# Ten root sums a layer on GpSimd, lagged sums on GpSimd, two mixer outputs parked in DRAM, and one squared root in the convolution

## The chip, the cores and the metric

The kernel runs on one core of one Trainium2 chip. The metric is the device time of one execution in microseconds (us). Three runs of the kernel before took 2062.20, 2062.73 and 2065.04 us; their median is 2062.73 us.

## The reference

A decoder trunk of two layers over 1024 tokens of width 1024, all in float32. Cut to what matters here (`norm` divides by the root of the mean square over the last axis):

```python
for l in range(2):
    h = rmsnorm(x, attn_norm[l])
    (c_q, c_kv, k_r, g_b, g_c, u_conv, u_pool, q_sw, k_sw, v_sw) = split(h @ w_in[l])
    y_a = mla_attention(c_q, c_kv, k_r, ...)      # RMSNorm of c_q and of c_kv inside
    y_b = g_b * conv3(g_c * u_conv)               # causal, depthwise, width 3
    y_c = pool(u_pool) @ pool_w * pool_scale      # trailing means over 2, 4, 8, 16 tokens
    y_d = swa_sink_attention(q_sw, k_sw, v_sw)    # window of 128 tokens
    mixed = concat(norm(y_a), norm(y_b), norm(y_c), norm(y_d)) * mix_norm[l]
    x = x + mixed @ w_o[l]
    gate, up = split(rmsnorm(x, ffn_norm[l]) @ w_gate_up[l])
    x = x + (silu(gate) * up) @ w_down[l]
return rmsnorm(x, final_norm)
```

## The kernel before

Channels lie on the 128 partitions, tokens on the free axis in two halves t of 512. To keep float32 accuracy, each operand of a product is split in two float32r parts (ScalarE casts the high part, VectorE subtracts it), and `mm3` (L260) issues three matmuls for each product of tiles. SBUF beside constants and temporaries is 47 slots of 128 x 1024 (`u`), handed out and taken back by `Slots`.

**One layer, in the order of the code.** The projections of the local attention (group d), the first half of the convolution (group b), the pooling (group c: its lagged sums are `lagged`, L770 to L785), the low-rank q and kv projections with their norms (`sq_q` at L822, `sq_kv` at L832), the second half of the convolution (`conv(1)`), which serves as TensorE work while the keys and queries of the main attention (group a) are made, then eight attention steps with pieces of the output projection (`out_some`) between them, then the feed-forward part.

**The norms.** The class `SumSq` (L298) squares tiles on ScalarE and adds them on VectorE. `rnorm` (L334) sums the result over the 128 partitions with a matmul against a matrix of ones: one plain float32 matmul (L343), or, with `pair=True`, the sum is first split in two and there are two float32r matmuls (L340). The product lies in PSUM on all partitions; three ScalarE operations (L349 to L351) and two of VectorE (L352, L355) make the inverse root. A layer has ten such sums inside the mixers: two halves each for groups b, c and d (`group_scale`, L673), for `sq_q` and for `sq_kv`. Of them b and kv use the pair. Group a, the two norms of x and the final norm use `rnorm` too.

**What sets the order.** Nothing runs in the order of the code. `scheduled_kernel` (L1972) traces the kernel, gives every instruction a cost (`Order.costs`), makes a list schedule for the five engines (PE, ScalarE, VectorE, GpSimd, SP with its DMAs), chooses PSUM banks from it, and fixes each engine's order by added dependencies. Each engine then takes its instructions strictly in that order: one that waits holds up all behind it. GpSimd runs the sums of feed-forward weights (L749 to L752 ahead of the attention, L1213 to L1243 and L1532 later), a multiplication in the gates (L1454) and small memsets (L1041).

Of the kernel before, what the change touches and what calls it, by code (L numbers as in the profile page):

```python
# [6 lines left out]

# [4 lines left out]

F32 = mybir.dt.float32
# [98 lines left out]
def trunk_kernel(ctx: ExitStack, tc: tile.TileContext, ins, out, given=None):  # L112
# [13 lines left out]
    def rd(ap):  # L126
        return ap.bitcast(F32)
# [170 lines left out]
    class SumSq:  # L298


        def __init__(self, n, pair=False):
            self.n, self.pair = n, pair
            self.acc = [None, None]
            self.done = {}
            self.held = {}
            self.hl = {}
# [27 lines left out]
        def rnorm(self, t, cols=whole, tag="t", final=None):  # L334

            a, n = F.ap(self.acc[t])[:, cols], self.n
            p = ps(tag)[:, cols]
            if t in self.hl:
                for i, h in enumerate(self.hl.pop(t)):
                    pe.matmul(p, ones_r, R.ap(h), start=i == 0, stop=i == 1)  # L340
                    R.free(h)
            else:
                pe.matmul(p, ones, a, start=True, stop=final is None)  # L343
# [8 lines left out]
            dve.scalar_tensor_tensor(  # L352
                out=q, in0=p, scalar=-0.5 / n, in1=q, op0=ALU.mult, op1=ALU.mult
            )
            dve.scalar_tensor_tensor(out=a, in0=q, scalar=1.5, in1=r0, op0=ALU.add, op1=ALU.mult)  # L355
            return self.acc[t]

    def mul_to(o, a, b):
# [2 lines left out]
    def pcol(l, c, rows=slice(0, P)):  # L361
        return par[rows, l * PC_N + c : l * PC_N + c + 1]
# [55 lines left out]
    for l in range(L):  # L418
# [115 lines left out]
        for t in range(2):  # L534
            f = tmp()
            mul_to(f, pk[t], r_of(t))
            for g, own, oth in ((0, hd, tl), (1, tl, hd)):
                k1, k2 = R.ap(kk[g][0] + t), R.ap(kk[g][1] + t)
                act.copy(k1[own], f[own])
                act.copy(k1[oth], f[own])  # L540
                dve.tensor_tensor(out=k2[own], in0=f[own], in1=rd(k1[own]), op=ALU.subtract)
                dve.tensor_tensor(out=k2[oth], in0=f[own], in1=rd(k1[own]), op=ALU.subtract)
        vs = [[R.half(), R.half()] for _ in range(2)]
        for t in range(2):
            f = tmp()
# [138 lines left out]

        mixed = {}

        def group_split(g, t):
            for c in range(2):
                s = y[g][c][t]
                mixed[g, c, t] = half_split(F.ap(s), pcol(l, PC_MIX + 2 * "abcd".index(g) + c))  # L690
                F.free(s)


        y["b"] = [None, None]

        def conv(ct):
# [13 lines left out]
            c = PC_CONV + ct  # L710
# [51 lines left out]
        for ct in range(2):  # L762
# [5 lines left out]
            nextp = project()  # L768

            def lagged(o, i, lag, rows=slice(0, P)):  # L770
                dve.tensor_copy(o[rows, :lag], i[rows, :lag])
                dve.tensor_tensor(
                    out=o[rows, lag:], in0=i[rows, lag:], in1=i[rows, : S - lag], op=ALU.add
                )

            lagged(af, uf, 1)
            if ct == 0:
                lagged(bf, af, 2, tl)
                dve.tensor_copy(bf[hd], af[hd])
                src, dst = bf, af  # L780
            else:
                lagged(bf, af, 2)
                lagged(af, bf, 4)
                lagged(bf, af, 8, tl)
                dve.tensor_copy(bf[hd], af[hd])  # L785
                src, dst = bf, af
            cf = CC_FIX + 16 * ct
            dve.scalar_tensor_tensor(
# [556 lines left out]
        for n, (h, t) in enumerate(steps):  # L1345
# [8 lines left out]
            if n == 0:  # L1354
# [450 lines left out]
class Order:  # L1805
# [74 lines left out]
    def costs(cls, i):  # L1880
# [320 lines left out]
```

## Time and profile before

| what | value |
|---|---|
| runs | 2062.20, 2062.73, 2065.04 us |
| span of the profiled execution, first to last instruction | 2061.2 us |
| median run less that span | 1.5 us |
| granted TensorE clock | 0.998 |
| mixers of layer 0 | about 0 to 235 us, attention steps to 440 us |
| mixers of layer 1 | about 1050 to 1235 us, attention steps to 1440 us |
| feed-forward parts | about 440 to 1050 us and 1440 to 2061 us |

The profile has no time of its own for the execution that it shows beside its span; what lies around the span is taken as the 1.5 us to the median. In its rows PE is TensorE, DVE VectorE, ACT ScalarE, POOL GpSimd and SP the queue that issues all DMAs. A row of instructions gives line, engine, operation, output<-inputs, shape, count, and busy time with the mean in ns. In the timeline a row begins with its start and its length in us. A float32 matmul stands as two records.

### The profile page before, as it was taken

How to read it: one execution, taken by the hardware profiler on the slowest of the kernel's cores; microseconds unless marked ns; L12 is line 12 of the kernel's file. 1: busy time of each engine (PE TensorE's matmuls, PEld its weight loads, DVE VectorE, ACT ScalarE, POOL GpSimd, SP SyncE). 2: the span in 40 equal slices, each digit the busy share in tenths (PEclk: the TensorE clock that was granted, in tenths of full speed). 3: DMA queues.
4: the chain of work that ended last, by engine and by line, in shares of the span. 5: the costliest groups of instructions: out<-in, count | busy, mean ns of one | idle time of the engine just before them, and what ended most of it. 6: DMA issues, size and time to landing. Idle time of an engine off the chain costs nothing.

```text
span 2061.2 us, 26597 instructions
## 1 busy us (share of the span) xinstructions
PE 2035.3 (99%) x9422; PEld 1673.6 (81%) x9422; DVE 1503.7 (73%) x2443; ACT 992.6 (48%) x1743; POOL 577.3 (28%) x420
## 2 busy tenths in 40 slices
PE   9999999999999999999999999999999999999998
PEld 7887888778888888888888878888788877788887
DVE  8779979987666667655657898889866655585555
ACT  7447657753333334444433666668433333354342
POOL 0200000037777773000002000000577777710000
PEclk9999999999999999999999999999999999999999
DMA  5211223334554556766413112142455555487642
GB/s 191 90 57 46 84 78 96 137 133 168 181 175 167 189 169 235 265 220 208 140 46 124 37 42 97 61 144 94 159 169 178 178 175 170 154 302 237 204 171 96
DMA packets 142118, 302.37 MB, mean 147 GB/s; under 512 B 13856, under 2 KB 60960, under 8 KB 141984
## 3 DMA queue, kind: packets, MB, share of 16 engines
q1 hardware_dynamic: 141984, 300.66, 43.1%
q8 instruction: 74, 1.21, 0.2%
q14 instruction: 60, 0.49, 0.1%
HBM read 212.00 MB, written 87.56 MB: 145 GB/s over the span
## 4 chain that ended last, share of the span: by engine, by line
PE 68%; POOL 7%; DVE 5%; DMA 4%; issue 2%; ACT 2%; SPq 0%; DVEq 0%; POOLq 0%; ACTq 0%
PE ps_mm L260 25%; PE ps_s L260 21%; PE ps_t L260 8%; PE ps_pv L260 6%; POOL u L1532 3%; PE ps_pv L1044 2%; PE ps_t L1032 1%; DMA u<-in_w_dn 1%; POOL tp L1454 1%; DMA ad<-u 1%; POOL u L1214 1%; DVE u L283 1%; POOL u L1213 1%; ACT u L280 1%; DMA u<-in_w_gu 1%
## 5 line engine op out<-in xcount | busy, mean ns | idle before, releaser
L260 PE MATMUL ps_mm<-u,u 128*128 128x512 f32 (+1 forms) x3378 | 831.0, 390 | 3.4 <-ACT u L280 2.3
L260 PEld LDWEIGHTS ps_mm<-u,u 128*128 128x128 f32 x3378 | 615.4, 188 | 130.4 <-issue 5.3
L260 PE MATMUL ps_s<-u,u 128*128 128x512 f32 x2670 | 636.1, 390 | 5.8 <-DVE tn L352 2.3
L283 DVE TENSOR_TENSOR u<-u,u 128x1024 fp32r<-128x1024 f32 (+2 forms) x400 | 443.3, 1126 | 225.2 <-ACT u L280 173.4
L260 PEld LDWEIGHTS ps_s<-u,u 128*128 128x128 f32 x2670 | 499.5, 188 | 117.8 <-ACT tn L1321 3.9
L280 ACT CAST u<-u 128x1024 fp32r<-128x1024 f32 (+2 forms) x400 | 345.1, 881 | 505.4 <-POOL u L1215 60.1
L260 PE MATMUL ps_t<-u,u 128*128 128x512 f32 (+1 forms) x1124 | 255.3, 378 | 2.8 <-DVE u L1447 2.7
L260 PEld LDWEIGHTS ps_t<-u,u 128*128 128x128 f32 x1124 | 201.6, 188 | 45.8 <-DVE u L1447 6.5
L1454 POOL TENSOR_TENSOR tp<-tp,u 128x512 f32<-128x512 f32 x80 | 135.1, 1689 | 341.7 <-ACT tp L1453 341.7
L260 PE MATMUL ps_pv<-u,u 128*128 128x512 f32 x744 | 177.8, 390 | 1.6 <-DVE te L1658 1.0
L260 PEld LDWEIGHTS ps_pv<-u,u 128*128 128x128 f32 x744 | 139.3, 188 | 32.1 <-ACT tn L1321 1.9
L1041 POOL MEMSET u<- 128x128 f32 x32 | 5.9, 211 | 472.9 <-PE ps_pv L1044 149.3
L1453 ACT ACTIVATE tp<-tp 128x512 f32<-128x512 f32 x80 | 50.5, 631 | 155.2 <-DVE tp L359 155.1
L749 POOL TENSOR_TENSOR u<-u,u 128x512 f32<-128x512 f32 x4 | 6.0, 1509 | 380.4 <-PE ps_t L622 288.9
L1532 POOL TENSOR_TENSOR u<-u 128x352 f32<-128x352 f32 x64 | 80.5, 1259 | 31.6 <-DMA u<-in_w_dn 30.2
L280 ACT CAST u<-ps_t 128x512 fp32r<-128x512 f32 (+3 forms) x132 | 65.1, 504 | 48.1 <-PE ps_t L1032 26.7
L1532 POOL TENSOR_TENSOR u<-u,u 128x352 f32<-128x352 f32 x64 | 85.0, 1328 | 3.0
L285 ACT ACTIVATE u<-u,par 128x512 fp32r<-128x512 f32 x100 | 70.6, 717 | 28.5 <-DVE u L359 11.1
L283 DVE TENSOR_TENSOR u<-ps_t,u 128x512 fp32r<-128x512 f32 (+3 forms) x132 | 75.9, 582 | 11.1 <-ACT u L280 9.8
L286 DVE SCALAR_TENSOR_TENSOR u<-u,par,u 128x512 fp32r<-128x512 f32 x100 | 73.7, 750 | 5.9 <-ACT u L285 5.9
L324 ACT ACTIVATE tn<-u 128x512 f32<-128x512 f32 (+1 forms) x91 | 52.3, 595 | 48.6 <-DVE u L1723 42.1
L359 DVE TENSOR_TENSOR tp<-tp,u 128x512 f32<-128x512 f32 x76 | 72.5, 954 | 2.0
(208 smaller groups left out, 2359.3 us busy)
## 6 DMA issues: line engine op xcount, KB each, us to landing
u<-in_w_gu SPq DMA_DIRECT2D x92, 512.0 KB, 4.1
ad<-u SPq DMA_DIRECT2D x154, 256.0 KB, 3.9
u<-ad SPq DMA_DIRECT2D x70, 512.0 KB, 5.1
u<-in_w_dn SPq DMA_DIRECT2D x64, 352.0 KB, 3.4
qd<-u SPq DMA_DIRECT2D x64, 352.0 KB, 2.4
u<-qd SPq DMA_DIRECT2D x32, 512.0 KB, 4.7
u<-in_w_in SPq DMA_DIRECT2D x28, 512.0 KB, 3.5
u<-in_w_dn SPq DMA_DIRECT2D x24, 512.0 KB, 5.2
```

What stands on the lines that cost most here:

```text
L260: pe.matmul(o, w, r, start=start and k == 0 and i == 0, stop=stop and k == n - 1 and i == 2, skip_group_check=again,)
L280: a = act.copy(hi, f)
L283: dve.tensor_tensor(out=lo, in0=f, in1=rd(hi), op=ALU.subtract)
L285: a = act.activation(hi, f, AF.Copy, scale=gain)
L286: dve.scalar_tensor_tensor(out=lo, in0=f, scalar=gain, in1=rd(hi), op0=ALU.mult, op1=ALU.subtract)
L324: act.activation(q, f, AF.Square)
L359: dve.tensor_tensor(out=o, in0=a, in1=b, op=ALU.mult)
L1032: pe.transpose(p[:, b * P : (b + 1) * P], pr[b][j // 4][:, (j % 4) * P : (j % 4 + 1) * P], ident,)
L1044: pe.matmul(py[:, c0:], v_of(j, h), R.ap(s)[:, c0:], start=j == 0 and n == 0, stop=j == nj - 1 and n == 1,)
L1453: last_silu = act.activation(g, g, AF.Silu)
L1454: pool.tensor_tensor(out=g, in0=g, in1=r, op=ALU.mult)
L1532: pool.tensor_tensor(out=o, in0=a, in1=b, op=ALU.add)
```

## The change

Six edits, all in the mixers.

1. `SumSq` gets a flag `pooled`. With it, `rnorm` sums over partitions with one GpSimd instruction (`partition_all_reduce`, 128 x 512, SBUF to SBUF, L340 of the changed kernel) in place of the matmuls. All ten sums a layer named above use it, and the splits for b and kv are gone with the pair.
2. `lagged` runs its additions on GpSimd and its copies on ScalarE, before on VectorE.
3. The local keys are needed on both halves of the partitions. The second copy was made by a ScalarE cast and a VectorE subtraction; now two SP DMAs copy the finished halves.
4. The split outputs of groups c and d go to DRAM (eight tiles of 512 KB a layer, L706), their slots become free, and `fetch_mixed` reads them back (L715) ahead of the output projection.
5. The convolution took (p1 r)(p2 r) with the root r in three VectorE products a half; now ScalarE squares r and VectorE takes two.
6. The scheduler's cost function gets a price for the new GpSimd instruction.

```diff
         def rnorm(self, t, cols=whole, tag="t", final=None):
             a, n = F.ap(self.acc[t])[:, cols], self.n
-            p = ps(tag)[:, cols]
-            if t in self.hl:
+            if self.pooled:
+                o = F.half()
+                p = F.ap(o)
+                pool.partition_all_reduce(p, a, P, bass_isa.ReduceOp.add)
+            else:
+                p = ps(tag)[:, cols]
+            if self.pooled:
+                pass
+            elif t in self.hl:
...
                 act.copy(k1[own], f[own])
-                act.copy(k1[oth], f[own])
                 dve.tensor_tensor(out=k2[own], in0=f[own], in1=rd(k1[own]), op=ALU.subtract)
-                dve.tensor_tensor(out=k2[oth], in0=f[own], in1=rd(k1[own]), op=ALU.subtract)
+                for k in (k1, k2):
+                    sp.dma_start(rd(k[oth]), rd(k[own]))
...
-            sg = SumSq(2 * P, g in "b")
+            sg = SumSq(2 * P, pooled=True)
...
+                    i = R.pair()
+                    split(R.ap(i), R.ap(i + 1), F.ap(s), gain)
+                    parked[g, c, t] = dpool.tile([P, 2 * HT], F32, name=f"mx{l}{g}{c}{t}")
+                    sp.dma_start(parked[g, c, t], rd(R.ap2(i)))
+                    R.free_pair(i)
...
+        def fetch_mixed():
+            for t in HALVES:
+                for g in "dc":
+                    for c in range(2):
+                        i = R.pair()
+                        sp.dma_start(rd(R.ap2(i)), parked[g, c, t])
+                        mixed[g, c, t] = i, i + 1
...
-                mul_to(F.ap(z + t), pp[t], r_of(t))
+                act.activation(F.ap(z + t), r_of(t), AF.Square)
+                mul_to(F.ap(z + t), pp[t], F.ap(z + t))
...
-                f = tmp()
-                mul_to(f, pp[t], r_of(t))
-                mul_to(F.ap(z + t), F.ap(z + t), f)
+                mul_to(F.ap(z + t), pp[t], F.ap(z + t))
...
-                dve.tensor_copy(o[rows, :lag], i[rows, :lag])
-                dve.tensor_tensor(
+                act.copy(o[rows, :lag], i[rows, :lag])
+                pool.tensor_tensor(
...
-        sq_q = SumSq(2 * P)
+        sq_q = SumSq(2 * P, pooled=True)
...
-        sq_kv = SumSq(P, True)
+        sq_kv = SumSq(P, pooled=True)
...
+                fetch_mixed()
                 values()
...
+            if op == "ISA":
+                return 0.4 + n * 0.00625, 0.4 + n * 0.00625
```

The scheduler orders the whole program anew. Three places matter below. On GpSimd in the mixers of layer 0, before: the sums of two sets of feed-forward weights (the last two rows here), and next the memsets of the attention.

```order
L752 TENSOR_TENSOR u_1042<-u_1042 128x512
L752 TENSOR_TENSOR u_1030<-u_1030 128x512
L1041 MEMSET u_2441 128x128 x2
L1041 MEMSET u_2653 128x128 x2
L1041 MEMSET u_2840 128x128 x2
```

The same place in the changed kernel. L796 is `lagged`; `ISA` without an operand loads another library of GpSimd code, and `ISA` with one is the new sum: first group c (1415, 1430), then kv (1748, 1765), then q (1476).

```order
L776 TENSOR_TENSOR u_1040<-u_1040 128x512
L796 TENSOR_TENSOR u_1108<-u_1107 128x1023
L796 TENSOR_TENSOR u_1109<-u_1108 64x1022
L796 TENSOR_TENSOR u_1258<-u_1257 128x1023
L796 TENSOR_TENSOR u_1259<-u_1258 128x1022
L796 TENSOR_TENSOR u_1258<-u_1259 128x1020
L796 TENSOR_TENSOR u_1259<-u_1258 64x1016
L340 ISA
L340 ISA u_1415<-u_1415 128x512
L340 ISA u_1430<-u_1430 128x512
L340 ISA u_1752<-u_1748 128x512
L340 ISA u_1769<-u_1765 128x512
```

Six additions, a library load and ten sums now stand where GpSimd had nothing to do; a second load (`ISA` at L1479) stands ahead of the first multiplication of the gates. Layer 1 has the same.

On TensorE in the mixers of layer 0, before, where the rotary key (L850) is projected: the two pair matmuls of kv's second half (L340) stand among its rows.

```order
L850 MATMUL ps_s<-u_352,u_1740 128x512 x2
L340 MATMUL ps_t<-u_1769,ones_r 128x512
L850 MATMUL ps_s<-u_364,u_1740 128x512 x2
L850 MATMUL ps_s<-u_376,u_1740 128x512
L340 MATMUL ps_t<-u_1769,ones_r 128x512
L850 MATMUL ps_s<-u_376,u_1740 128x512
L260 MATMUL ps_mm<-u_156,u_1837 128x512 x2
```

The same place in the changed kernel, where the line of the rotary key is L874 and L891 is the copy of its rotated rows.

```order
L891 MATMUL ps_t<-u_1802,e_r 128x512
L874 MATMUL ps_s<-u_352,u_1744 128x512
L874 MATMUL ps_s<-u_364,u_1744 128x512 x2
L874 MATMUL ps_s<-u_376,u_1744 128x512
L891 MATMUL ps_t<-u_1802,e_r 128x512
L874 MATMUL ps_s<-u_376,u_1744 128x512
L260 MATMUL ps_mm<-u_156,u_1834 128x512
```

The ones matmuls are gone from the row, and the projection of `conv(1)` still follows.

On the SP queue at the start of the attention steps, before: L194 loads rows of `w_o`, L199 the weights of queries and L1099 loads x.

```order
L194 DMA u_2177<-in_w_o 128x768
L199 DMA vraw<-in_w_uq 128x256 x2
L1099 DMA u_2312<-in_xT 128x512
L199 DMA vraw<-in_w_uq 128x256
L1099 DMA u_2451<-in_xT 128x512 x2
L194 DMA u_2494<-in_w_o 128x768
```

The same stretch in the changed kernel, where L706 parks a tile of group d, L715 fetches one, and x is loaded at L1123.

```order
L715 DMA u_2220<-mx0c_1463 128x1024
L706 DMA mx0d_1975<-u_1972 128x1024
L715 DMA u_2214<-mx0d_1975 128x1024
L706 DMA mx0d_1980<-u_1977 128x1024
L715 DMA u_2218<-mx0c_1458 128x1024
L706 DMA mx0d_1965<-u_1962 128x1024
L715 DMA u_2216<-mx0d_1980 128x1024
L706 DMA mx0d_1970<-u_1967 128x1024
L1123 DMA u_2319<-in_xT 128x512
L194 DMA u_2176<-in_w_o 128x768
L715 DMA u_2206<-mx0d_1965 128x1024
L199 DMA vraw<-in_w_uq 128x256
```

Each fetch of a tile of d stands close behind the store of the same tile, and the loads of x, of `w_o` and of query weights stand behind both.

More of the change, by code (lines that the diff above doesn't have):

```diff
@@ L9 @@
 import concourse.tile as tile
-from concourse import mybir
+from concourse import bass_isa, mybir
 from concourse._compat import with_exitstack
@@ L298, in trunk_kernel, with __init__ @@
     class SumSq:
-        def __init__(self, n, pair=False):
-            self.n, self.pair = n, pair
+        def __init__(self, n, pair=False, pooled=False):
+            self.n, self.pair, self.pooled = n, pair, pooled
             self.acc = [None, None]
@@ L355, in rnorm @@
             dve.scalar_tensor_tensor(out=a, in0=q, scalar=1.5, in1=r0, op0=ALU.add, op1=ALU.mult)
+            if self.pooled:
+                F.free(o)
             return self.acc[t]
@@ L683, in group_scale @@
                 F.free(r)
-        mixed = {}
+        mixed, parked = {}, {}
         def group_split(g, t):
@@ L689, in group_split @@
                 s = y[g][c][t]
-                mixed[g, c, t] = half_split(F.ap(s), pcol(l, PC_MIX + 2 * "abcd".index(g) + c))
-                F.free(s)
+                gain = pcol(l, PC_MIX + 2 * "abcd".index(g) + c)
+                if g == "b":
+                    mixed[g, c, t] = half_split(F.ap(s), gain)
+                else:
+                    i = R.pair()
[3 more added lines that the diff above has]
+                    R.free_pair(i)
+                F.free(s)
+        def fetch_mixed():
[5 more added lines that the diff above has]
+                        mixed[g, c, t] = i, i + 1
         y["b"] = [None, None]
@@ L778, in trunk_kernel @@
                 lagged(bf, af, 2, tl)
-                dve.tensor_copy(bf[hd], af[hd])
+                act.copy(bf[hd], af[hd])
                 src, dst = bf, af
@@ L784, in trunk_kernel @@
                 lagged(bf, af, 8, tl)
-                dve.tensor_copy(bf[hd], af[hd])
+                act.copy(bf[hd], af[hd])
                 src, dst = bf, af
```

## The prediction

> **What bounds the kernel now.** I read the page's first part, then the busy time by stage, then TensorE's waits, then the chain that ended last.
>
> ```profile
> span 2061.2 us, 26597 instructions
> PE 2035.3 (99%) x9422; PEld 1673.6 (81%) x9422; DVE 1503.7 (73%) x2443; ACT 992.6 (48%) x1743; POOL 577.3 (28%) x420
> ```
>
> TensorE has something in flight for 2035.3 of 2061.2 us; no other engine comes near. An average can hide a stage with another limit, so here are the mixers and the attention steps of both layers (PE, PEld, DVE, ACT and POOL busy, clock, DMA share, GB/s).
>
> ```profile
> 0.00:110.00 110.00, 107.38 (x508) 87.17 (x509) 88.01 (x186) 63.87 (x132) 11.17 (x12) 1.00 0.41 144
> 110.00:235.00 125.00, 124.89 (x597) 101.44 (x596) 114.38 (x252) 78.34 (x173) 0.35 (x2) 1.00 0.14 45
> 235.00:440.00 205.00, 200.26 (x975) 163.12 (x974) 180.12 (x375) 141.08 (x281) 9.00 (x18) 1.00 0.31 106
> 1110.00:1235.00 125.00, 125.00 (x591) 101.48 (x590) 110.39 (x232) 72.78 (x155) 11.70 (x8) 1.00 0.18 61
> 1235.00:1440.00 205.00, 204.26 (x1015) 169.14 (x1014) 182.70 (x390) 140.82 (x292) 6.89 (x17) 1.00 0.30 100
> ```
>
> From 110 to 235 and from 1110 to 1235 us, where the ten sums of each layer lie, TensorE is never seen idle, at the full clock. VectorE is the next (114.38 and 110.39 of 125), GpSimd all but empty (0.35 and 11.70). The waits of TensorE name nothing of size in the mixers:
>
> ```profile
> PE ps_t L260 <- DVE u L1447: 2.7, 7, 1.2
> PE ps_s L260 <- DVE tn L352: 2.3, 1, 2.3
> PE ps_mm L260 <- ACT u L280: 2.3, 2, 1.5
> ```
>
> So there the end is set by how much TensorE has to do: what is taken from its row comes off the end, unless something new makes it wait.
>
> **What leaves TensorE.** The records of the ones matmuls, the pace of float32r matmuls in the chain of waits, and one float32 sum in the timeline with what follows it:
>
> ```profile
> L343 PE MATMUL ps_t<-u,ones x28: 590/592/697, 19.9 to 1216.5; 128*128 128x512 f32 x28
> L340 PE MATMUL ps_t<-u,ones_r x24: 389/392/504, 174.4 to 1377.4; 128*128 128x512 f32 x24
> ...
> 500.49 2.72 PE ps_mm L260 x12
> ...
> 197.85 1.02 PE L343 MATMUL ps_t<-u,ones 128*128 128x512 f32 x2
> 198.31 4.66 PE L260 MATMUL ps_mm<-u,u 128*128 128x512 f32 x18
> 202.81 0.51 PE L978 MATMUL ps_s<-u,u 128*128 128x384 f32 x2
> ```
>
> Busy times of pipelined matmuls overlap, so I price by starts. A float32r matmul of 512 columns takes 2.72 / 12 = 0.227 us. From 197.85 to 202.81 are 4.96 us; the 18 float32r ones are 4.08, so the float32 sum took 0.88. The 28 float32 records are 14 sums; two belong to the norm of x at the entry and stay, so 12 go (c, d and q, two halves, two layers): 12 x 0.88 = 10.5 us. Of the 24 float32r records 8 are group a's and stay, 16 go (b and kv): 16 x 0.227 = 3.6 us. **TensorE loses 14.1 us.** No matmul is added.
>
> **The new sum on GpSimd.** No trace row shows it. The nearest rows are GpSimd's additions over the same 512 columns:
>
> ```profile
> L749 POOL TENSOR_TENSOR u<-u,u 128x512 f32<-128x512 f32 x4 | 6.0, 1509 | 380.4 <-PE ps_t L622 288.9
> ...
> L1454 POOL TENSOR_TENSOR tp<-tp,u 128x512 f32<-128x512 f32 x80 | 135.1, 1689 | 341.7 <-ACT tp L1453 341.7
> ```
>
> One pass over the data takes 1.5 us, the lower bound. If 128 partitions are folded in seven halvings, each such a pass, it is 7 x 1.51 = 10.6 us, the upper. I take 4 us, nearer to the row: a single instruction over the same columns, with some exchange between partitions. What matters is when its result is late. The tightest user is kv, whose result leads to the first keys:
>
> ```profile
> 170.51 0.42 DVE L319 TENSOR_SCALAR u<-u 128x512 f32<-128x512 f32 x1
> 174.93 0.42 DVE L319 TENSOR_SCALAR u<-u 128x512 f32<-128x512 f32 x1
> ...
> 187.40 0.74 DVE L286 SCALAR_TENSOR_TENSOR u<-u,par,u 128x512 fp32r<-128x512 f32 x1
> ...
> 193.68 0.63 PE L260 MATMUL ps_s<-u,vhi 128*128 128x512 f32 x2
> ...
> L280 ACT CAST u<-u 128x512 fp32r<-128x512 f32 x87 | 53.9, 621 | 137.0 <-POOL u L1243 56.9 <-DVE u L798 23.2 <-PE ps_s L260 18.6
> L283 DVE TENSOR_TENSOR u<-u,u 128x512 fp32r<-128x512 f32 x87 | 71.0, 819 | 27.6 <-ACT u L280 27.5
> ```
>
> The two sums of squares of kv are ready at 170.93 and 175.35 (L319 ends); the last split behind the second root ends at 188.14 (L286); the first keys start at 193.68. Spare: 5.5 us. The pair's cast, subtraction and two matmuls leave this path: 0.62 + 0.82 + 2 x 0.227 = 1.9. So the second sum may take until 175.35 + 7.4 = 182.8 before TensorE waits. The two sums stand in line on GpSimd, so with t for each the second ends at 170.93 + 2t (for t over 4.4), and TensorE waits 2t - 11.9 us a layer from t = 5.9 on. With 4 us it waits for nothing; the cover is the projection of `conv(1)`, which runs there anyway. The sums of c come earlier, those of d and b go to the output projection, and q's stand behind kv's: at 4 us the first is done by 183 and the scores start at 202.81. I take 0.
>
> The Trainium skill (GPSIMD Engine Reference, Cross-partition) states 247,699 ns for a `tensor_reduce` along partitions at 128 x 2048. A quarter of it for 512 columns would be 62 us, an estimate; the formula would then add 2 x (124 - 11.9) = 224 us and give some 2275. No run so far shows either instruction.
>
> **The library loads.** Each layer gets two. The one that the kernel has already lies somewhere in GpSimd's first 91 us of idleness and shows no cost. The first new one stands between the last lagged sum and the sum of c, 20 us ahead of kv's; the second stands ahead of the gates, where GpSimd waits for ScalarE anyway (L1454 row above, 341.7 us idle in all). I take 0. The Trainium skill (GPSIMD Engine Reference, Instruction dispatch) adds about 6 us to the first call after a load; covered in the same way it changes nothing, and no row of this trace shows it.
>
> **The other edits**, with their rows:
>
> ```profile
> L772 DVE TENSOR_TENSOR u<-u 128x1023 f32<-128x1023 f32 x4 | 4.9, 1223 | 0.1
> L542 DVE TENSOR_TENSOR u<-te,u 64x512 fp32r<-64x512 f32 x8 | 5.5, 687 | 0.1
> L359 DVE TENSOR_TENSOR te<-ps_mm,u 128x512 f32<-128x512 f32 x39 | 26.8, 687 | 16.5 <-PE ps_mm L260 16.2
> L359 DVE TENSOR_TENSOR tp<-tp,u 128x512 f32<-128x512 f32 x76 | 72.5, 954 | 2.0
> ```
>
> VectorE loses 12 lagged sums at 1.22 (14.6 us), 8 second key copies at 0.687 (5.5), 8 products of the convolution at 0.687 (5.5) and 8 subtractions of the pairs at 0.82 (6.6): 32 us over both layers. ScalarE loses 16 casts and gains 8 squares, 4 copies of half the partitions and some small ones, about even. VectorE is not the bound there (114.38 of 125), so this relief is worth between 0 and the 2.6 us that TensorE idles in the first 110 us; I take 0. Some of it is given back: VectorE's products of two SBUF tiles take 954 ns in the gates, where GpSimd runs at the same time, and 687 from PSUM.
>
> The lagged sums become longer: the second channel tile has four in a row, 1.22 us each on VectorE, twice 1.51 = 3.0 us on GpSimd. That is 7.1 us later a layer for the pooling's matmuls, which stand in TensorE's fixed row with everything behind them. The order was made anew for slower sums, so most of it is covered by projections; left is what contention adds. Between 0 and 7.1 a layer I take 0.5.
>
> The parked tiles and key copies on the SP queue:
>
> ```profile
> u<-u SPq DMA_DIRECT2D x8, 128.0 KB, 2.3
> gd<-u SPq DMA_DIRECT2D x8, 512.0 KB, 4.4
> u<-gd SPq DMA_DIRECT2D x4, 512.0 KB, 3.6
> ...
> 209.11 0.75 DVE L286 SCALAR_TENSOR_TENSOR u<-u,par,u 128x512 fp32r<-128x512 f32 x1
> ...
> 245.64 4.88 PE ps_mm L260 x20
> ```
>
> The last split of d ends at 209.86; a fetch of d waits for the landing of its store (4.4) and lands 3.6 later, and behind it on SP wait the loads of x, `w_o` and query weights. Four such turns in a line are 4 x (4.4 + 3.6) = 32 us; the first long run of output projections starts at 245.64, 35.8 after the split. It just fits, and the turns overlap in part. Between 0 and 4.4 a layer (one store) I take 0.5. The key copies land 2.3 us after issue in place of 1.3 on two engines; the projections of q and of the convolution stand in between: 0.
>
> **Sum.** -14.1 + 2 x (0.5 + 0.5) = -12.1 us on the span of 2061.2, so 2049.1, and with the 1.5 around it **2050.6 us**.
>
> **The rivals.** A measurement of this kernel can tell about 0.2% (4.1 us) from no change: faster is below 2058.6, slower above 2066.9.
>
> *The slow sum (slower).* If a sum takes t over 5.9 us, the keys wait 2t - 11.9 us a layer. From t = 9.0 the gain is gone, from t = 10.1 the change is slower; at the upper bound of 10.6 the wait is 9.3 a layer, 2050.6 + 18.6 = 2069.2. For it: ten sums on one engine in line, and a fold over partitions is more than a pass. Against: 5.5 us of spare are seen, and the one-pass row is 1.5 us. Chance 0.10, its page-priced extreme among it at 0.02.
>
> *The late lagged sums (same).* If the slower chain is not covered, TensorE waits up to 7.1 us a layer at the pooling's matmuls: -14.1 + 14.2 + 1 gives 2063.8. For it: TensorE's row is fixed, and VectorE and GpSimd slow each other. Against: the local attention's matmuls and projections are there to run. Chance 0.10.
>
> *The queue behind the parked tiles (same or a little faster).* If the turns of store and fetch do not fit, x, `w_o` and query weights come late by up to one store for each of two tiles, 8.8 us a layer: -14.1 + 17.6 + 1 gives 2067.2 at the end, half of it 2058.4. For it: 32 against 35.8 us. Against: the DMA engines are at 0.31 there. Chance 0.06.
>
> *More than the sum.* If the relief of VectorE ends TensorE's small waits as well, 2.6 us of the start and most of the 4.7 from 235 to 440 us go: 2050.6 - 7.3 = 2043.3. Chance 0.06.
>
> The slots that the parked tiles free could also be no use, since d's are fetched straight back; that changes no term.
>
> **The numbers.** My forecast, 2044 to 2058, has the chance 0.68. The range goes from 2043.5 (relief) up to 2063 (the late sums): outside lie the slow sum, and the ends of the others, about 0.18. Faster: 0.68 + 0.06 + half of the queue's and part of the late sums' case, 0.80. Same: 0.10. Slower: 0.10.
>
> **What would show it.** In the profile of the changed kernel L343's successor has 4 records on `ps_t` in place of 28, the pair 8 in place of 24, and TensorE's busy time in the two stretches of mixers falls by about 7 us each, with no new releaser above 1 us. The new rows of GpSimd should have a mean near 4 us; above 6 us the keys (`ps_s` with `vhi`) should wait for VectorE behind GpSimd. A wait of the pooling's `ps_t` matmuls for a split behind L796 would show the late sums, one of output projections for an SP load the queue. I am wrong if TensorE's row is 14 us shorter and the span is not.

## The result, and the profile after

The changed kernel takes 2101.1 us (median of four runs, 2100.71 to 2101.32), the kernel before on the same chip 2063.89 (2062.2 to 2065.23): a ratio of 1.0178, 95% interval 1.0166 to 1.019. The forecast was 2050.6. It is slower by 37 us where I said faster by 12.

The first lines of the page of the changed kernel:

```profile
span 2099.4 us, 26643 instructions
PE 2043.0 (97%) x9382; PEld 1678.0 (80%) x9382; DVE 1515.1 (72%) x2391; ACT 995.0 (47%) x1751; POOL 669.7 (32%) x452
```

The span is 38.2 us longer. TensorE was without work for 25.9 us before (2061.2 - 2035.3) and is for 56.4 now (2099.4 - 2043.0): 30.5 us more. Its mean granted clock (the share of full speed at which TensorE was allowed to run) fell from 0.998 to 0.990; by the span that is 21.0 us lost now and 4.1 before, 16.9 more. Against these stand the 14.1 us of ones matmuls. 30.5 + 16.9 - 14.1 is 33.3; some 5 us of the 38.2 stay unassigned in this sum. The same stages as in the prediction (PE, PEld, DVE, ACT and POOL busy, clock, DMA share, GB/s):

```profile
0.00:110.00 110.00, 107.36 (x508) 87.46 (x509) 85.81 (x179) 62.35 (x131) 12.67 (x12) 1.00 0.45 153
110.00:235.00 125.00, 113.63 (x513) 91.58 (x512) 108.38 (x201) 69.63 (x153) 40.60 (x15) 0.95 0.24 83
235.00:440.00 205.00, 198.71 (x967) 161.69 (x966) 180.30 (x382) 137.99 (x285) 12.18 (x19) 0.99 0.34 114
1110.00:1235.00 125.00, 116.10 (x553) 95.99 (x552) 103.07 (x220) 66.97 (x161) 42.12 (x19) 0.95 0.23 81
1235.00:1440.00 205.00, 198.84 (x987) 164.98 (x986) 183.81 (x387) 132.20 (x282) 20.22 (x21) 0.99 0.38 127
```

In the two mixer stretches TensorE was busy for 124.89 and 125.00 of 125 us at the full clock; now it is for 113.63 and 116.10, at 0.95. In the same time it got through 513 records where it had 597. GpSimd went from 0.35 to 40.60 us in the first. VectorE, relieved of 16 us of work a layer, is still busy for 108.38 where it had 114.38, so what is left takes it longer. What TensorE waits for (total us, times, longest):

```profile
PE ps_t L631 <- DVE tp L620: 12.9, 7, 4.1
PE ps_mm L260 <- DVE u L935: 4.1, 2, 2.9
PE ps_mm L260 <- DVE u L368: 3.6, 2, 2.5
PE ps_s L874 <- DVE u L216: 2.7, 1, 2.7
```

All four name VectorE; no wait of TensorE names GpSimd or a DMA. L620 is a scaling of the local attention's weights in place (`tp`, SBUF to SBUF), which has nothing to do with any norm. Nor is the new instruction slow. Its group on GpSimd, a group of lagged sums, and the ones matmuls that are left:

```profile
L340 POOL PARTITION_ALL_REDUCE u<-u x20 | 68.1, 3412 | 152.2 <-DVE u L326 32.6 <-DVE u L368 24.0 <-DVE sm L615 21.5
L796 POOL TENSOR_TENSOR u<-u 128x1023 f32<-128x1023 f32 x4 | 7.6, 1894 | 28.5 <-DVE u L368 16.2 <-PE ps_t L260 12.2
...
L347 PE MATMUL ps_t<-u,ones_r 128*128 128x512 f32 x8 | 3.2, 416 | 0.0
L350 PE MATMUL ps_t<-u,ones 128*128 128x512 f32 x4 | 2.0, 592 | 0.0
```

3.4 us a sum, below the 4 that I took. What changed is VectorE. Here are groups from 110 to 260 us of the kernel before, and then the same instructions of the changed one (busy us and mean ns behind the bar):

```profile
L203 DVE TENSOR_TENSOR u<-u,u 128x1024 fp32r<-128x1024 f32 x5 | 6.1, 1223 | 4.7 <-PE ps_mm L260 4.4 <-ACT u L202 0.3
L611 DVE TENSOR_SCALAR tp<-tp,sm 128x256 f32<-128x256 f32 x14 | 4.4, 349 | 0.1
L286 DVE SCALAR_TENSOR_TENSOR u<-te,par,u 128x512 fp32r<-128x512 f32 x4 | 3.0, 744 | 0.0
L283 DVE TENSOR_TENSOR u<-ps_t,u 128x512 fp32r<-128x512 f32 x13 | 8.9, 686 | 0.9 <-ACT u L280 0.8
```

```profile
L203 DVE TENSOR_TENSOR u<-u,u 128x1024 fp32r<-128x1024 f32 x5 | 11.7, 2345 | 4.6 <-PE ps_mm L260 4.6
L620 DVE TENSOR_SCALAR tp<-tp,sm 128x256 f32<-128x256 f32 x14 | 7.4, 566 | 0.1
L286 DVE SCALAR_TENSOR_TENSOR u<-te,par,u 128x512 fp32r<-128x512 f32 x4 | 4.6, 1161 | 0.0
L283 DVE TENSOR_TENSOR u<-ps_t,u 128x512 fp32r<-128x512 f32 x8 | 5.5, 683 | 1.2 <-ACT u L280 1.2
```

Instructions with all their operands in SBUF take up to twice as long in the mean; the one that reads PSUM (L283) takes what it took. A mean hides that some instructions are held and others not at all. The timeline of the changed kernel (start, length), first three sums beside VectorE, then a lagged sum with the wait of TensorE behind it:

```profile
177.68 3.23 POOL L340 PARTITION_ALL_REDUCE u<-u  x1 [12.26 <-DVE u L319]
182.90 6.82 POOL L340 PARTITION_ALL_REDUCE u<-u  x2 [1.98 <-DVE u L319]
...
177.44 2.63 DVE L620 TENSOR_SCALAR tp<-tp,sm 128x256 f32<-128x256 f32 x2
179.99 0.68 DVE L326 SCALAR_TENSOR_TENSOR u<-tn,u 128x512 f32<-128x512 f32 x1
...
181.80 0.68 DVE L283 TENSOR_TENSOR u<-ps_t,u 128x512 fp32r<-128x512 f32 x1
...
183.33 3.26 DVE L203 TENSOR_TENSOR u<-u,u 128x1024 fp32r<-128x1024 f32 x1
186.51 0.41 DVE L660 TENSOR_TENSOR u<-ps_pv,tn 64x256 f32<-64x256 f32 x1
186.85 2.43 DVE L286 SCALAR_TENSOR_TENSOR u<-te,par,u 128x512 fp32r<-128x512 f32 x1
...
131.14 2.32 POOL L796 TENSOR_TENSOR u<-u 64x1016 f32<-64x1016 f32 x1 [1.21 <-ACT u L795]
...
131.20 2.54 DVE L620 TENSOR_SCALAR tp<-tp,sm 128x128 f32<-128x128 f32 x2
...
133.69 0.45 PE L631 MATMUL ps_t<-cst,tp 128*128 128x128 f32 x1 [4.03 <-DVE tp L620]
```

L203 needs 1.22 us and took 3.26 beside the first of the two sums at 182.90; then a product from PSUM runs at its 0.41; then L286, 0.74 otherwise, takes 2.43 beside the second.

In the whole trace 20 of VectorE's instructions with tensors in SBUF alone begin in the first 2 us of a sum (reciprocals of a column or two and register reads aside): all 20 are held, and none of the 14 that have an operand in PSUM is. (In the five other kernels with whole sums, run below, 83 of 87 are held.) The hold ends before the sum's record does. Less their usual time, the 20 go on 2.1 to 2.7 us after the sum began, while its record lasts 3.2 to 3.9; L326, SBUF alone, runs at its usual 0.68 from 179.99, and the record of the sum goes on to 180.91. Records of GpSimd are rough, so how much of that last microsecond is the record's is not shown.

At 131.20 two scalings of 0.28 us each took 2.54 beside a lagged sum, and TensorE's transposes, fixed in its order, wait 4.03 us for them. What follows such a wait shows in windows of 5 us of the same kernel:

```profile
125.00:130.00 5.00, 4.66 (x20) 3.28 (x18) 4.93 (x10) 3.11 (x12) 4.10 (x2) 1.00 0.00 0
130.00:135.00 5.00, 1.31 (x5) 1.16 (x6) 4.59 (x10) 0.47 (x3) 2.32 (x1) 0.77 0.01 3
135.00:140.00 5.00, 5.00 (x19) 4.23 (x19) 2.85 (x8) 3.03 (x9) 0.00 (x0) 0.55 0.00 0
```

TensorE is busy for 1.31 us of five, and the clock falls to 0.77 and 0.55. In the last row TensorE counts as fully busy, at little over half speed. A wait need not be that long: the same kernel has two more stretches of half clock in layer 0, from 180.5 and from 248.7 us, behind waits of 1.83 and 1.69 us in stretches of 3.4 us in which TensorE was busy for 1.16 and 1.54.

### The profile page after: what moved, and what is told of

Read it like the earlier page. It is cut to its first block, busy times and chain, and to the rows that moved or that the text cites. A ratio compares the mean times of both kernels' runs of the same rounds, so it can differ in the third digit from the quotient of the medians.

```text
span 2099.4 us, 26643 instructions
## 1 busy us (share of the span) xinstructions
PE 2043.0 (97%) x9382; PEld 1678.0 (80%) x9382; DVE 1515.1 (72%) x2391; ACT 995.0 (47%) x1751; POOL 669.7 (32%) x452
## 5 line engine op out<-in xcount | busy, mean ns | idle before, releaser
L283 DVE TENSOR_TENSOR u<-u,u 128x1024 fp32r<-128x1024 f32 (+2 forms) x392 | 434.3, 1125 | 228.2 <-ACT u L280 169.6
L280 ACT CAST u<-u 128x1024 fp32r<-128x1024 f32 (+2 forms) x392 | 340.4, 887 | 485.9 <-POOL u L1267 64.2
L1479 POOL TENSOR_TENSOR tp<-tp,u 128x512 f32<-128x512 f32 x80 | 134.8, 1686 | 341.2 <-ACT tp L1478 341.2
L340 POOL PARTITION_ALL_REDUCE u<-u x20 | 68.1, 3412 | 152.2 <-DVE u L326 32.6
L283 DVE TENSOR_TENSOR u<-ps_t,u 128x512 fp32r<-128x512 f32 (+3 forms) x132 | 75.1, 580 | 12.4 <-ACT u L280 11.5
L286 DVE SCALAR_TENSOR_TENSOR u<-u,par,u 128x512 fp32r<-128x512 f32 x100 | 74.9, 763 | 5.6 <-ACT u L285 5.3
```

The source lines that it names most:

```text
L280: a = act.copy(hi, f)
L283: dve.tensor_tensor(out=lo, in0=f, in1=rd(hi), op=ALU.subtract)
L286: dve.scalar_tensor_tensor(out=lo, in0=f, scalar=gain, in1=rd(hi), op0=ALU.mult, op1=ALU.subtract)
L340: pool.partition_all_reduce(p, a, P, bass_isa.ReduceOp.add)
L1479: pool.tensor_tensor(out=g, in0=g, in1=r, op=ALU.mult)
```

## The experiments

**The theories.** H, the hold: while a GpSimd instruction works on SBUF, VectorE's instructions with all operands in SBUF wait; TensorE waits for VectorE in its fixed order and then loses clock. Rivals: D, the later result (the roots wait for GpSimd); Q, the parked tiles' queue; L, the lagged sums on GpSimd and nothing else, late or holding; and N, the order that is left without the ones matmuls. Medians are in us; the kernel before lay between 2063.9 and 2065.4 on the chips of these runs.

**1. Which edit?** The changed kernel with the sums back on TensorE (edit 1 undone):

```diff
-        sq_kv = SumSq(P, pooled=True)      # and likewise sq_q and group_scale
+        sq_kv = SumSq(P, True)
```

> The changed kernel with edit 1 undone: the ten sums a layer are ones matmuls on TensorE again (with the pairs for b and kv), edits 2 to 5 stay. Theory H: a running GpSimd instruction holds up VectorE's instructions whose operands all lie in SBUF, and the 3.4 us sums cost most of it (held VectorE time in the trace of the changed kernel: 32 us behind the sums, 12 us behind the lagged sums). Then the 14.1 us of TensorE work come back, but most of the new waits go: 2066 to 2082 us. Rival Q (the parked tiles and key copies delay the SP queue): the loss stays, 2095 us or more plus the 14. Rival N (the new order is bad by itself): no forecast, about 2100.

2077.27, ratio 1.0056 (1.0041 to 1.0071), in H's range: 24 us of the 37 are gone with the sums, and Q, with all tiles still parked, had said 2095 or more. The kernel before with edit 1 (and 6) alone:

> The kernel before with edit 1 alone (and its price in the scheduler). Theory H: -14.1 us of TensorE work and the holds of the sums without any relief of VectorE: 2075 to 2100 us. Rival Q: the loss was of the parked tiles, so 2050 us. Rival L (the lagged sums on GpSimd are the cause, late or holding): 2050 to 2055 us.

2102.12, ratio 1.0179 (1.0163 to 1.0194), just above H's range. That it equals the whole change is chance, though. This kernel has a wait of its own, for the cast of a weight tile that was loaded late (timeline of TensorE):

```profile
1263.17 1.22 PE L260 MATMUL ps_mm<-u,u 128*128 128x512 f32 x2 [14.93 <-ACT u L202]
```

The sums take a slot each for their result, and without the parked tiles slots may be short. That is not shown: a large wait of this kind is absent wherever tiles are parked, but the kernel with idle sums (experiment 2) takes the same slots without parking, and its waits of this kind are 1.8 us in all. Why the tile is late stays open. The changed kernel with the lagged sums back on VectorE (edit 2 undone), and with edits 1 and 2 undone:

> The changed kernel with edit 2 undone: lagged sums and their copies on VectorE again. Theory H: 12 us of held VectorE time go, 15 us of work come back to it; the holds of the sums stay: 2080 to 2100 us. Rival L: 2050 to 2060 us. Rival Q: about 2100 us.

> The changed kernel with edits 1 and 2 undone: only the key copies by DMA, the parked tiles and the squared root stay. Theory H: no new GpSimd work, VectorE relieved by 11 us: 2058 to 2066 us. Rival Q: the loss of about 37 us or more stays, 2095 us or more. Rival L and H agree here.

2089.1, ratio 1.0116 (1.0101 to 1.0132), as H said and 29 above the most that L allowed, and 2069.92, ratio 1.0026 (1.0015 to 1.0037), above H's 2066 and far under Q's 2095: the three small edits gain nothing and cost 5 us.

**2. The hold or the later result?** First GpSimd's sums without use: the kernel before, whose roots still take the ones matmuls' result, with the ten sums a layer as extras.

```diff
                 p = ps(tag)[:, cols]
+                if self.extra:
+                    o = F.half()
+                    pool.partition_all_reduce(F.ap(o), a, P, bass_isa.ReduceOp.add)
```

> The kernel before, with its ones matmuls and all other edits undone, plus the ten sums a layer on GpSimd, written to a spare slot that nobody reads. Theory H (while GpSimd runs a sum, VectorE's instructions with all operands in SBUF stand still, TensorE waits for them and loses its clock): slower though nothing reads a result and TensorE has lost no work, 2085 to 2120 us, with granted clock near 0.99. Rival D (the roots wait for a sum's result, since GpSimd is slower than a ones matmul): nothing waits for these sums, so within 0.3% of the kernel before, 2062 to 2070.

2088.81, ratio 1.0121 (1.0107 to 1.0135). Nobody reads a result, TensorE does all its old work, and the kernel loses 25 us. Added up over its trace, what VectorE's instructions beside these sums take beyond the shortest of the same kind is 27 us, about the loss. Its stretches of mixers:

```profile
110.00:235.00 125.00, 118.10 (x545) 93.87 (x544) 115.76 (x232) 72.11 (x155) 32.01 (x11) 0.99 0.13 41
1110.00:1235.00 125.00, 118.95 (x565) 95.44 (x564) 108.14 (x228) 67.66 (x152) 33.17 (x15) 0.99 0.20 67
```

One tie is left: the root is written over the squares, so that this write waits for the sum. Then the reverse, a result as late without GpSimd, on the kernel with edit 1 alone:

```diff
-                pool.partition_all_reduce(p, a, P, bass_isa.ReduceOp.add)
+                sp.dma_start(p, a)
```

> The sums edit alone on the kernel before, but GpSimd's instruction is replaced by a DMA on the SP queue that copies the 128 x 512 squares as they are to the same slot (2 to 3 us, so the sum over partitions is left out; the roots wait for the copy as they would for the sum). TensorE has lost the ones matmuls, the result is about as late, and GpSimd does nothing. Theory H: the forecast gain appears, 2045 to 2056. Rival D (it is the later result): slow like the sums on GpSimd, 2085 to 2105.

2088.05, ratio 1.0112 (1.0096 to 1.0127), in D's range and against H. Its waits name another cause for a good part of it: 19.2 us, the longest 13.5, are for ACT u L202, the late weight tile again. Without them it would be some 2069, an estimate, still above H's range. So this run does not separate the two; the test was repeated on the changed kernel, where the parked tiles leave slots, with a ScalarE copy (no lateness, no hold) and with the DMA copy (lateness, no hold):

```diff
-                pool.partition_all_reduce(p, a, P, bass_isa.ReduceOp.add)
+                act.copy(p, a)             # or sp.dma_start(p, a)
```

> The changed kernel with each GpSimd sum replaced by a copy on ScalarE (0.6 us; the sum over partitions is left out). All other edits stay, TensorE has lost the ones matmuls, and the roots get their input at once. If the loss is what the sums do on GpSimd (hold or lateness): the kernel with the sums on TensorE and the rest of the change (2077.3) less the 14 us of the ones matmuls, 2056 to 2070. If the loss comes from the order that is left without the ones matmuls: 2085 to 2105.

> The changed kernel with each GpSimd sum replaced by a DMA copy of 128 x 512 on the SP queue (2.2 us from issue to landing; the sum over partitions is left out). The result is about as late as the sum's, GpSimd holds nobody for it, and the parked tiles keep their slots free, which the sums edit alone lacked. Hold: as with the copy on ScalarE, 2056 to 2072. Lateness: near the changed kernel, 2085 to 2105. Both in like parts: 2072 to 2085.

2060.41, ratio 0.9976 (0.9966 to 0.9986), and 2067.13, ratio 1.0005 (0.9996 to 1.0014). Against the changed kernel's 2101.1 the ScalarE copy gives 40.7 us, the DMA copy 34.0. N is out. The DMA's copy lands 2.3 us after its issue, ScalarE's takes 0.6, and the 1.7 us between them cost 6.7. The sum's 3.4 us are later than both; at the same price its 2.8 us beyond ScalarE's copy would cost 11 of the 40.7, an estimate. Some 30 are left to what only GpSimd's work does, near the 25 of the idle sums. Stretches of the kernel with the DMA copy:

```profile
110.00:235.00 125.00, 116.44 (x558) 95.34 (x557) 105.94 (x224) 79.42 (x174) 12.52 (x8) 0.99 0.39 131
...
1110.00:1235.00 125.00, 120.90 (x581) 99.68 (x580) 104.27 (x213) 75.11 (x159) 24.34 (x14) 1.00 0.35 123
```

TensorE is still not full there (116.44; the lagged sums are still on GpSimd), but the clock stays at 0.99 and 1.00, where the changed kernel had 0.95 in both.

**3. Does the forecast gain exist?** The ScalarE copy, and the lagged sums back on VectorE, so that nothing new runs on GpSimd:

> The changed kernel with the lagged sums back on VectorE and each GpSimd sum replaced by a copy on ScalarE (the sum over partitions is left out): nothing new on GpSimd in the mixers. If the 14 us of the ones matmuls come off the end: the kernel with neither edit (2069.9) less 14, 2053 to 2059. If half of them are lost again on the way: 2060 to 2066. Beside the same kernel with the lagged sums on GpSimd (2060.4) it gives what those cost without the sums: 0 to 7 us.

2054.35, ratio 0.9947 (0.9932 to 0.9962). Beside the kernel with the sums on TensorE and all else alike but for the 20 copies (2069.92) that is 15.6 us, where I had 14.1. Its stretches:

```profile
110.00:235.00 125.00, 122.11 (x597) 101.04 (x597) 115.55 (x256) 88.74 (x194) 0.35 (x2) 1.00 0.34 117
...
1110.00:1235.00 125.00, 124.67 (x606) 103.53 (x605) 112.41 (x240) 83.00 (x176) 11.49 (x10) 1.00 0.39 136
```

Now the 37 us can be walked in four steps, each between two measured kernels: before 2064.6, edits 3 to 5 to 2069.9 (+5.3), the ones matmuls off TensorE to 2054.4 (-15.6), the sums on GpSimd to 2089.1 (+34.8), the lagged sums on GpSimd to 2101.1 (+12.0). Twenty sums at 34.8 are 1.7 us each, half of the 3.4 for which one runs. The 34.8 holds what the later result costs too. The held time that the trace of the changed kernel shows on VectorE (expectation of experiment 1) is near both last steps: 32 us behind the sums and 12 behind the lagged ones.

**4. The form of the hold.** Each sum in four instructions of 128 columns, on the kernel with edit 1 alone:

```diff
-                pool.partition_all_reduce(p, a, P, bass_isa.ReduceOp.add)
+                for k in range(0, HT, P):
+                    pool.partition_all_reduce(p[:, k : k + P], a[:, k : k + P], P, bass_isa.ReduceOp.add)
```

> The sums edit alone on the kernel before, each sum issued as four of 128 columns. Theory H, form 1 (VectorE waits for the end of the running GpSimd instruction and gets in between two): holds become shorter, mean of a held 128x512 product below 1.5 us, and the time falls under that of whole sums, 2070 to 2095. H, form 2 (what counts is how long GpSimd is busy in all, which grows by the fixed cost of four instructions): not less than with whole sums, 2100 to 2125.

2112.0, ratio 1.0234 (1.022 to 1.0248), the range of the second form, but the time is inconclusive: TensorE waits 31.0 us for the late weight tiles here (two waits, the longest 18.0), 18.3 with whole sums. The rows of VectorE tell more. First a group from 110 to 260 us with whole sums (experiment 1, edit 1 alone), then the same group with quarters; the kernel before has 683 ns. The last row is the quarters' group on GpSimd and gives a price by size:

```profile
L368 DVE TENSOR_TENSOR u<-u,u 128x512 f32<-128x512 f32 x15 | 13.3, 906 | 0.0
...
L369 DVE TENSOR_TENSOR u<-u,u 128x512 f32<-128x512 f32 x14 | 10.0, 744 | 0.1
...
L341 POOL PARTITION_ALL_REDUCE u<-u x80 | 95.8, 1269 | 208.1 <-DVE sm L618 90.2 <-DVE u L326 62.7 <-DVE u L286 16.7
```

A held 128 x 512 product takes 0.9 to 1.1 us here and up to 2.7 beside whole sums, and the held time over the whole trace is 10 us, 25 with whole sums. That is the sign of the first form: VectorE gets in between two instructions. That the kernel becomes faster by it is not shown.

Then the sums of q and kv back on TensorE, those of c, d and b kept on GpSimd:

> The changed kernel with the four sums a layer of q and kv back on TensorE; c, d and b stay on GpSimd (6 of 10 sums). If each sum costs alike: six tenths of the way from the kernel with all sums on TensorE (2077) to the changed one (2101), 2088 to 2095. If the sums cost where they meet the local attention's steps (c, q and kv lie there, d and b later): nearer to all on TensorE, 2077 to 2086.

2087.38, ratio 1.011 (1.0094 to 1.0125), between the two expectations. Against all sums on TensorE (2077.27) it is 10 us dearer with 12 sums, the whole change 24 with 20: the 12 of c, d and b cost, and the 8 of q and kv more each.

**5. Can the order hide it?** The planner of the kernel before already lengthens a VectorE instruction with two operands in SBUF while a GpSimd addition runs (`SHARED = 0.6`, L1813 and L1971). The new sum was given a duration and not this mark, so the order of the changed kernel was made as if it held nobody. Now the planner was told of the hold:

```diff
+                if kind[k] == "sum":
+                    held = t + seen
+                elif kind[k] in ("one", "two") and held > t:
+                    seen, taken = held - t + seen, held - t + taken
```

> The changed kernel, its instructions as they are, but the planner that writes the order is told that VectorE's instructions with all operands in SBUF wait for the end of a running GpSimd sum. If the loss is an order made with wrong durations: most of it comes back, 2055 to 2080. If the mixers have no room for the held time whatever the order: 2088 to 2105.

2099.14, ratio 1.0169 (1.0152 to 1.0185): no difference from the changed kernel that the intervals tell. With the hold in its durations (to the end of a sum, longer than the trace shows) this list schedule finds no better place; that none exists is not shown, since it places each engine's next instruction greedily.

**6. The small edits, one at a time** (squared root, key copies, parked tiles, each alone on the kernel before):

> The kernel before with one edit alone: the convolution's square of the root on ScalarE (8 products fewer on VectorE, 8 squares more on ScalarE). If VectorE's relief is worth nothing where TensorE sets the end: within 0.2% of the kernel before, 2060 to 2067. If it is this edit that costs what the three small edits together cost (some 5 us): 2067 to 2072. If VectorE's relief counts: 2055 to 2060.

> The kernel before with one edit alone: the second halves of the local keys copied by DMA in place of ScalarE and VectorE. If the SP queue takes them without harm: within 0.2% of the kernel before, 2060 to 2067. If their place on the queue makes loads late: 2067 to 2072.

> The kernel before with one edit alone: the split tiles of a, c and d parked in DRAM and fetched back. As forecast (half a microsecond a layer): within 0.2% of the kernel before, 2060 to 2067. If the turns of store and fetch make loads late, one store a layer or two: 2068 to 2080. It should carry what the small edits together cost (some 5 us), as neither the root nor the key copies do.

2066.16, ratio 1.0012 (1.0003 to 1.0021); 2063.19, ratio 0.9993 (0.9984 to 1.0002); 2067.07, ratio 1.001 (1.0001 to 1.002). (The third parks c and d, as the change does, not a.) Together they would make 1.0015, and the three at once made 1.0026 (1.0015 to 1.0037), so the two differ by no more than the intervals allow. Each lies within 0.2%; no single one carries the 5 us.

**7. A version without GpSimd.** The kernel before with the key copies by DMA, and with all sums as float32r pairs:

```diff
-            sg = SumSq(2 * P, g in "b")
+            sg = SumSq(2 * P, True)
...
-        sq_q = SumSq(2 * P)
+        sq_q = SumSq(2 * P, True)
```

> A version with no sum on GpSimd: the kernel before with the key copies by DMA and with all five sums of a half as float32r pairs on TensorE (c, d and q as well, 12 sums in two layers). TensorE gives 12 x (0.88 - 0.454) = 5.1 us; ScalarE and VectorE get 12 casts and 12 subtractions more. If it comes off the end: 2056 to 2061, faster than both kernels. If VectorE's extra steps are late in the mixers: 2062 to 2070.

2069.12, ratio 1.0022 (1.0013 to 1.0032): 0.2% slower, in the second range. The reading, which no run takes apart, is that TensorE's 5 us do not pay for VectorE's 12 more steps in a stage where VectorE is the next bound. So the other way, fewer steps on both: the last addition of the squares writes float32r at once, and one float32r matmul sums it.

```diff
                 dve.scalar_tensor_tensor(
-                    out=a, in0=q, scalar=e, in1=a, op0=ALU.add, op1=ALU.add
+                    out=o, in0=q, scalar=e, in1=a, op0=ALU.add, op1=ALU.add
                 )                          # o: a float32r slot, R.ap(h)
```

> A version with no sum on GpSimd: the kernel before with the key copies by DMA, and the squares of all five groups rounded once to float32r where VectorE makes them, so that each of the 20 sums is one float32r matmul (this changes the rounding of the squares, not what is computed). TensorE gives 12 x (0.88 - 0.227) for c, d and q and 8 x 0.227 for b and kv, 9.6 us; ScalarE and VectorE lose the 8 casts and 8 subtractions of the pairs. If what TensorE gives comes off the end where nothing new is put on GpSimd: 2051 to 2058, faster than both kernels. If the order takes it back: 2060 to 2068.

2050.27, ratio 0.993 (0.9918 to 0.9942): 15 us faster than the kernel before, 51 faster than the changed one. The squares lose their low float32r part; the rest is the reference as before. Its ones matmuls and its stretches:

```profile
L351 PE MATMUL ps_t<-u,ones_r 128*128 128x512 f32 x28 | 11.5, 415 | 0.2 <-DVE u L283 0.2
```

```profile
110.00:235.00 125.00, 123.70 (x604) 102.07 (x603) 116.00 (x257) 81.54 (x181) 0.35 (x2) 1.00 0.16 48
1110.00:1235.00 125.00, 123.56 (x595) 101.92 (x595) 110.10 (x237) 73.78 (x158) 6.66 (x6) 1.00 0.20 62
```

## Why the prediction was wrong

- **What bounds the kernel: right.** In the mixers TensorE set the end, and with nothing new on GpSimd the 14.1 us came off it (15.6 measured, experiment 3). The records of the ones matmuls fell to 4 and 8 as stated.
- **The price of a sum: right, 3.4 us for 4.** The slow-sum rival (from 5.9 us on) is refuted by the L340 row (its bound for slower, 10.1, comes out at 10.0). So is the 62 us worked out from the Trainium skill (GPSIMD Engine Reference, Cross-partition), which speaks of another instruction.
- **"What matters is when its result is late": wrong, the step that failed.** I followed the sum's result to its users and asked nothing of what the instruction does beside it. Sums that nobody reads cost 25 us; a copy that is late by 2.3 us without GpSimd costs 6.7 more than one of 0.6. The term put at 0 for the sums is 34.8 us, most of it the hold, and that for the lagged ones 12.0 in place of 1.
- **"Some of it is given back": seen, not priced.** I quoted the row that shows the effect, VectorE's products in the gates at 954 ns beside GpSimd for 687 otherwise. That mean comes from a stage where GpSimd's instructions take 1.7 us and TensorE has other matmuls queued. Priced for the mixers it would have been: GpSimd gets ten sums of 4 us and six lagged sums of 3 a layer, 58 us by my own prices, about a stretch where VectorE is busy for 114 of 125; if half of that time VectorE stands, 29 us, its 11 us of spare and the 16 of relief are gone. The kernel's planner carried a price for the same effect (experiment 5), and I did not ask why the new instruction had none.
- **VectorE's relief "taken as 0": the wrong question.** It was worth nothing as a gain (edits 3 to 5 alone, with 11 of its 32 us, cost 5 us), but it was the room that the hold would use up.
- **The lagged sums: size and mechanism off.** 1 us in two layers was forecast; measured are 6.1 (without sums on GpSimd, 2060.41 less 2054.35), 7.4 (sums on TensorE, 2077.27 less 2069.92) and 12.0 (sums on GpSimd). The rival had the pooling's matmuls waiting for late lagged sums; these were shorter than thought (1.89 to 2.32 us for 3.0), and the wait is that of the local attention for VectorE, held by them.
- **Parked tiles, key copies, library loads: near enough.** No TensorE wait names a DMA. Parking alone costs 0.1% where 0.05% was forecast. A sum of c starts at 154.59, 0.25 us after its squares are done (L326 at 153.65 for 0.69), so no load delays it.
- **"Wrong if TensorE's row is 14 us shorter and the span is not"** named the right failure, but not how it came. TensorE lost the 40 records of ones matmuls, and its busy time still rose, from 2035.3 to 2043.0 us, since part of it ran at half clock: a wait of TensorE costs its length, and then often clock. The mean clock is 0.990 with sums and lagged sums on GpSimd, 0.993 with the sums alone and 0.998 with neither, where it was before.

That a running GpSimd instruction holds VectorE is shown by the rows (20 of 20 in the changed kernel, and none of 14 from PSUM) and by the idle sums; it fits all runs but the two that the late weight tiles spoil (the DMA copy and the quarters, both on the kernel with edit 1 alone). The Trainium skill (SBUF — State Buffer, section "SBUF: two separate sides") states it as a rule: the two share a pair of ports under an exclusive lock, held for the whole instruction, and a VectorE instruction with two SBUF inputs, or in a two-port mode, is blocked. The trace agrees in kind (L203 at 3.26 us for 1.22, L283 from PSUM unchanged), and the scaling L620, with one tensor input, is held as well (2.54 us for two of 0.28). It does not show a hold for the whole instruction: VectorE goes on about 1 us before a sum's record ends (179.99 against 180.91). I had not weighed that rule, and it is the one that spoke against this change.

On the clock, the Trainium skill (TensorE: Matmul & The Clock Gate, Part 1) has half rate after an idle window of about 3.4 us. The 4.03 us wait followed by 0.77 and 0.55 agrees; the waits of 1.83 and 1.69 us do not, as half clock follows them too, and in the kernel with the ScalarE copies a wait of 3.49 us from 129.36 is followed by 1.00.

What stays open: whether the three small edits cost more together than each alone, how the 34.8 divide between hold, later result and clock, why the weight tiles come late with edit 1 alone, what decides that a wait is followed by half clock, and whether an order exists in which the sums lie only beside PSUM work.

## What to carry to other kernels

Work moved to an idle engine is not free because that engine is idle: ask which other engine it stops while it runs. Where this hold shows, add GpSimd's time on SBUF to VectorE's time on SBUF-only instructions, as one budget for the stage (a bound: here a sum of 3.4 us held VectorE for 2.1 to 2.7 at most), and look at a stage where both run already for the price. When the aim is to relieve TensorE, look first for a cheaper form of the same matmul: rounding the squares once (9.6 us of TensorE off by estimate, 15 at the end) beat moving them.

## What the runs showed of the hardware

- PARTITION_ALL_REDUCE over 128 x 512 in float32 takes 3.41 us, over 128 columns 1.27: some 0.56 us and 5.6 ns a column, by these two.
- In the changed kernel each VectorE instruction with all its tensors in SBUF (small reciprocals aside) that began in the first 2 us of a GpSimd sum went on only 2.1 to 2.7 us after the sum's start and then took its usual time: 1.22 us becomes 3.26, 0.74 becomes 2.43. A product from PSUM between them takes its usual 0.41.
- A GpSimd addition of 1023 columns from two shifted views of one tile took 1.89 us (2.22 and 2.32 in two other groups of lagged sums); one of 512 columns from two tiles takes 1.51 in the kernel before.
- In the changed kernel waits of TensorE of 1.69 to 4.05 us are followed by stretches of half clock of 3.4 to 6.8 us, in which its row reads as fully busy; a wait of 3.49 us in another run is not.
